# The second layer's second feed-forward chunk: from a plain product to seven products, with its weights' sums made behind the root's logarithm

## The chip, the cores and the metric

The kernel runs on one core of a Trainium2 chip. The metric is the device time of one execution in microseconds (us). TensorE (PE) multiplies, VectorE (DVE) and ScalarE (ACT) do the elementwise work, GpSimd (POOL) issues the adding transfers, SyncE (SP) issues all other loads and stores.

## The reference, cut to what matters

An encoder of two layers runs on 768 tokens (512 and 256) of width 1024. Behind each layer's mixer comes a feed-forward part:

```python
h = rms_norm(x, norm_mlp[i])
x = x + jnp.square(jax.nn.relu(h @ mlp_w_up[i])) @ mlp_w_down[i]
```

`mlp_w_up` is 1024 x 4096, everything is float32. `rms_norm` multiplies each token by one over the root of its mean square; the kernel applies that factor (`rstd`) behind the product, since it is the same for all of a token's columns.

## The kernel before

All data stand with channels on the 128 partitions and the 768 tokens along the free dimension. A float32 operand is split in two parts, a rounded high part (`hi`, made by ACT) and the rest (`lo`, made by DVE as source minus `hi`), and a product is the sum of three: hi by hi, hi by lo, lo by hi. A low part can also be made by an adding transfer: ACT writes -hi into `lo`, and a transfer from POOL's queue adds the source to it (`Weights7.added`).

The feed-forward part works in 16 chunks `u` of 256 hidden units, and `mlp` lists its jobs: chunks 0, 1 and 2, then `down` products and further chunks in turns. A chunk has two raw tiles of weights of 128 x 1024, `raw[0]` and `raw[1]`, loaded by SP into three `wraw` buffers. A chunk's product has two forms:

- *plain* (`up_plain`, `up_begun`): two outputs `p1` and `p2` of 768 tokens, each 48 matmuls of 384 columns, 96 in all. `up_begun` is the first chunk; its two outputs enclose the sum of squares `ss`, the logarithm `ln` and the steps to `rstd`.
- *seven products* (`up`): weights and inputs are each taken as 2 x 2 blocks, and seven products of 12 matmuls do what eight do. They need sums of the blocks: `sums32` and `sums14` make the weights' (two DVE steps each, into tiles `sum0` and `sum1`), `Sums` made the inputs' earlier (`t`). The seven are, in order, `w11` (into bank `a`), `s3` (`b`), `s2` (into `a` again), `w12` (`c`), `s1`, `w22` (`d`) and `s4`. Between `w11` and `s2` ACT copies `a` to `c`, since the `w12` product continues from that, while `s2` goes on adding to `a`.

`PLAIN` says for each layer how many chunks are plain, 2 and 2. `Weights7.high` makes a group's high part on ACT and `low` the low part on DVE. Groups are `direct` (w11, w12), `second` (w21, w22), `s32` (s3, s2; tiles `zhi`, `zlo`), `s14` (s1, s4) and `w22` (`vhi`, `vlo`). PSUM has four banks of tag A, two of B and two of C.

What becomes of a chunk behind its product stands in `pend`, a list of steps that `late` issues inside the next chunk: squaring `y`, the parts `act` of it, and its sums `t`. Inside `mlp` the order on PE, DVE and ACT is the order in which this code is written (`manual_schedule`), and each engine works strictly through its own list. Multiplication by `rstd` with the rectifier is `rectified`, a DVE step `y<-p,rstd_mlp`.

Of the kernel before, what the change touches and what calls it, by code (L numbers as in the profile page):

```python
# [11 lines left out]
F32 = mybir.dt.float32  # L12
F32R = mybir.dt.float32r
AF = mybir.ActivationFunctionType
ALU = mybir.AluOpType
# [32 lines left out]
def trunk_kernel(ctx: ExitStack, tc: tile.TileContext, a: dict, out: bass.AP):  # L48
    nc = tc.nc
    act, dve, pe = nc.scalar, nc.vector, nc.tensor  # L50
# [31 lines left out]
    def split(hi, lo, src):  # L82

        first = act.activation(hi, src, AF.Copy)
        dve.tensor_tensor(lo, src, hi.bitcast(F32), ALU.subtract)
        return first.ins
# [23 lines left out]
    def fresh(name="mm", n=1, tag=None):  # L110

        nonlocal shift
        if tag is None:
            shift += 1
            tag = "ACAB"[shift % 4]
        return bank(tag, name) if n == 1 else [bank(tag, name) for _ in range(n)]

    def both(name="mm", tag=None):

        return [t[:, :H] for t in fresh(name, 2, tag)]  # L120
# [29 lines left out]
    def slot(i, name, dt=F32R, n=T):  # L150

        return (slots if i < 32 else more).tile([P, n], dt, tag=f"S{i}", name=name)

    def big(name, dt=F32):

        nonlocal turn
        if more is None:
            return tmp.tile([P, T], dt, tag="t", name=name)
        turn += 1
        return tmp.tile([P, T], dt, tag=f"q{turn % 6}", name=name, bufs=1)  # L160
# [174 lines left out]
    class Sums:  # L335
# [26 lines left out]
        def low(self, i):  # L362
            hi, lo = self.t[i]
            dve.tensor_tensor(lo[:], (self.q1, self.q2)[i][:], hi[:].bitcast(F32), ALU.subtract)

        def added(self, i):

            hi, lo = self.t[i]
            act.activation(lo[:], hi[:].bitcast(F32), AF.Copy, scale=-1.0)
            nc.gpsimd.dma_start(lo[:], (self.q1, self.q2)[i][:], accum_op=ALU.add)  # L370
# [34 lines left out]
    class Weights7:  # L405
# [44 lines left out]
        def added(self, group):  # L450

            self.high(group)
            self.due.remove(group)
            hi, lo, _ = self.parts[group]
            act.activation(lo[:], hi[:].bitcast(F32), AF.Copy, scale=-1.0)
            src = self.src[group != "direct"]
            nc.gpsimd.dma_start(lo[:], src[:, src.shape[1] - lo.shape[1] :], accum_op=ALU.add)

        def low(self, group):
            if group not in self.due:  # L460
# [477 lines left out]
    def up_chunk(l, u):  # L938
        f = 4 * (u // 2) + u % 2
        return Weights7(a["up"][l, f], a["up"][l, f + 2], plain=u < PLAIN[l])  # L940


    PLAIN = 2, 2

    def weave(*chains):

# [98 lines left out]
    def mlp(l, norm, nxt, w, places, early, product=None, begun=None):  # L1045
# [11 lines left out]
        def squared(t):  # L1057
            act.activation(t[:], t[:], AF.Square)  # L1058

        def acts_of(u, y1, y2, rest):  # L1060

            own = places[7 * (u % 2) : 7 * (u % 2) + 7]
            e = Acts(y1, y2, own, groups[u // 2], u % 2)
            if u < 2 * NG - 2:
                return [
                    lambda: squared(rest),
                    lambda: e.highx(0),
                    lambda: (e.highx(1), e.lowx(0), e.lowx(1), e.t13()),
                    e.t42,
                    lambda: e.high(0),  # L1070
                    lambda: e.high(1),
                    lambda: e.low(0),
                    lambda: e.low(1),
                ]

            def whole(i, q):
                hi, lo = slot(own[2 * i], "act"), slot(own[2 * i + 1], "act")
                split(hi[:], lo[:], q[:])
                groups[u // 2].setdefault("whole", {})[u % 2, i] = hi[:], lo[:]

            return [lambda: squared(rest), lambda: whole(1, y2), lambda: whole(0, y1)]
# [22 lines left out]
        def up_begun(u, w, make, then):  # L1104


            nonlocal r
            v, parts, *sums = begun
            ps = [both(f"p{i + 1}", "A") for i in range(2)]
            if sums:  # L1110
                return up_first(ps, w, v, parts, *sums)
            plain_block(ps[0], 0, w)
            ss = norm.sum_squares(psum, parts=parts, tag="C")
            logs, newton, result = norm.rstd_steps(psum, ss)
            logs()
            v.split("direct")
            newton()
            result()
            r = norm.r
            y = [big(f"y{i + 1}") for i in range(2)]  # L1120
            for i in range(2):
                if i:
                    plain_block(ps[1], 1, w)
                for o in range(2):
                    rectified(y[i], ps[i][o], H * o, H * o + H, ALU.max)
                if i == 0:
                    squared(y[0])
            pend.extend(acts_of(u, *y, y[1]))
            return v

        def up_first(ps, w, v, parts, s1):


            nonlocal r
            plain_block(ps[0], 0, w, range(4))
            ss = norm.sum_squares(psum, parts=parts, tag="C")
            plain_block(ps[0], 0, w, range(4, KB))
            plain_block(ps[1], 1, w)
            logs, newton, result = norm.rstd_steps(psum, ss)
            logs()  # L1140
            s1.t13()
            s1.t42()
            s1.high(0)
            s1.high(1)
            newton()
            s2 = norm.copied(2, 6)
            result()
            r = norm.r
            v.high("direct")
            s1.low(0)  # L1150
            s1.low(1)
            s2.t13()
            s2.high(0)
            v.low("direct")
            v.added("second")
            s2.t42()
            s2.high(1)
            s3 = norm.copied(3, 7)
            s2.low(0)
            s2.low(1)  # L1160
            y = [big(f"y{i + 1}") for i in range(2)]
            for i in range(2):
                for o in range(2):
                    rectified(y[i], ps[i][o], H * o, H * o + H, ALU.max)
                if i == 0:
                    s3.t13()
                    s3.high(0)
                    squared(y[0])
                    s3.added(0)
                    s3.t42()  # L1170
                    s3.high(1)
            pend.extend(acts_of(0, *y, y[1]))
            aside.append(lambda: s3.added(1))
            return v
# [93 lines left out]
        def up(u, w, make, then):  # L1268


            first = u == PLAIN[l]
            w.low("s32")
            w.split("s14")
            if not first:
                late()
            v = make()
            seven = isinstance(v, Weights7)
            a = bank("A", "a")[:, :H]
            product7(a, w, "w11", xs, True)
            if not first:  # L1280
                late()
            c = bank("A" if first else "C", "c")[:, :H]
            act.activation(c, a, AF.Copy)
            late(5 if first else 1)
            w.split("w22")
            late()
            b = bank("A" if first else "B", "b")[:, :H]
            product7(b, w, "s3", xs, True)
            p = big("p")[:, :H]
            act.activation(p, b, AF.Copy)  # L1290
            if seven:
                v.sums32()
            product7(a, w, "s2", xs, False)
            d = bank("B", "d")[:, :H]
            act.activation(d, a, AF.Copy)
            late(2)
            if seven:
                v.sums14()
                v.high("s32")
            late()  # L1300
            product7(c, w, "w12", xs, False)
            if seven:
                v.high("direct")
            product7(a, w, "s1", xs, False)
            y1, y2 = big("y1"), big("y2")
            dve.tensor_tensor(y2[:, H:], a, p, ALU.add)  # L1306
            rectified(y1, c, 0, H, ALU.max)
            late()
            if seven:
                v.low("direct")  # L1310
            else:
                v = [then(0)]
            product7(d, w, "w22", xs, False)
            if seven:
                v.added("w22")
            dve.tensor_tensor(y2[:, :H], d, p, ALU.add)
            rectified(y2, y2[:], 0, T, ALU.min)
            squared(y2)
            product7(a, w, "s4", xs, False)
            rectified(y1, a, H, T, ALU.max)  # L1320
            pend.extend(acts_of(u, y1, y2, y1))
            return v
# [74 lines left out]

        ups = [(up if u >= PLAIN[l] else up_plain, u) for u in range(2 * NG)]
        if begun:
# [585 lines left out]
```

## Time and profile before

| | |
|---|---|
| time, median of 3 runs | 1660.08 us (1659.68 to 1662.16) |
| profiled execution | 1661.51 us, its span 1659.5 us |
| granted TensorE clock, mean | 0.996 |
| busy share | PE 99%, DVE 83%, ACT 57%, POOL 4% |
| layer 2, first chunk | PE from 1098.1 us |
| layer 2, second chunk | PE from 1115.5 to 1132.2 us |
| layer 2, third chunk | PE from 1132.2 to 1146.9 us |

The profile is of one execution. Times of rows count from the start of its span. A row of an engine's order in time gives start, length, engine, source line, operation, output<-input, shape and how many follow each other; in brackets stands how long the engine was idle ahead of it and what ended that. The line is that of `kernel.py` before. PE's rows overlap, as one matmul starts before the last has ended.

### The profile page before, as it was taken

The numbers are of one execution on the slowest core, as the hardware profiler recorded it, in microseconds if no ns is written. First come the engines' busy times: TensorE is split into PE (matmuls) and PEld (weight loads), VectorE is DVE, ScalarE is ACT, GpSimd is POOL, SyncE is SP. The second block draws the span as 40 slices with busy tenths as digits, with TensorE's granted clock in tenths as the row PEclk, the third lists the DMA queues.
The fourth block names the chain that finished last, engine by engine and source line by source line (L and its number), as shares of the span: only waits on it lengthen the run. The fifth ranks groups of instructions, "written<-read, shape, count | busy, mean of one in ns | idle before, by whom it ended". The sixth has DMA issues, their size and how long they took to land.

```text
span 1659.5 us, 24297 instructions
## 1 busy us (share of the span) xinstructions
PE 1637.6 (99%) x9414; PEld 1587.3 (96%) x9414; DVE 1380.8 (83%) x2242; ACT 948.5 (57%) x1508; POOL 71.7 (4%) x104
## 2 busy tenths in 40 slices
PE   8999999999999999999999999999999999999997
PEld 7988789999999999999999999999999999999986
DVE  7598888898889889877888777778889888988776
ACT  7377766865556556545654434555555655655554
POOL 0211000000000000000000000000000000000000
PEclk9999999999999999999999999999999999999998
DMA  8755322443233333242312222112333323333222
GB/s 267 199 154 149 87 64 83 121 109 87 83 86 96 96 96 91 71 122 69 98 62 77 76 77 76 64 64 73 87 96 96 95 87 79 90 96 108 69 87 99
DMA packets 55476, 161.11 MB, mean 97 GB/s; under 512 B 7056, under 2 KB 10128, under 8 KB 55360
## 3 DMA queue, kind: packets, MB, share of 16 engines
q1 hardware_dynamic: 45184, 139.89, 26.4%
q0 software_dynamic: 10176, 19.67, 6.7%
q8 instruction: 74, 1.21, 0.3%
q14 instruction: 42, 0.34, 0.1%
HBM read 138.82 MB, written 10.48 MB: 90 GB/s over the span
## 4 chain that ended last, share of the span: by engine, by line
PE 88%; DVE 7%; ACT 4%; issue 1%; DMA 0%; DVEq 0%; SPq 0%; ACTq 0%
PE a L486 33%; PE mm L131 10%; PE mm L140 8%; PE b L486 8%; PE d L486 5%; PE c L486 5%; PE B L486 4%; PE C L486 4%; PE gate L140 3%; PE pt L760 1%; PE p L1096 1%; PE p L1199 1%; PE gate L131 1%; PE O L770 1%; PE O L771 1%
## 5 line engine op out<-in xcount | busy, mean ns | idle before, releaser
L486 PE MATMUL a<-xs,whi 128*128 128x384 f32 x624 | 121.8, 337 | 0.0
L444 ACT ACTIVATE vhi<-wraw 128x512 fp32r<-128x512 f32 x67 | 42.2, 631 | 132.3 <-PE B L486 87.9
L486 PEld LDWEIGHTS a<-xs,whi 128*128 128x128 f32 x624 | 110.0, 188 | 0.2 <-DVE y L1306 0.2
L486 PE MATMUL a<-t,zhi 128*128 128x384 f32 x536 | 109.1, 337 | 0.0
L486 PE MATMUL a<-t,whi 128*128 128x384 f32 x536 | 108.8, 336 | 0.0
L486 PE MATMUL b<-t,zhi 128*128 128x384 f32 x536 | 108.7, 336 | 0.0
L1341 DVE TENSOR_TENSOR x<-x,a 128x384 f32<-128x384 f32 x112 | 62.1, 554 | 55.3 <-PE a L486 55.3
L486 PE MATMUL a<-act,whi 128*128 128x384 f32 x448 | 96.5, 337 | 0.0
L486 PEld LDWEIGHTS a<-t,whi 128*128 128x128 f32 x536 | 94.9, 188 | 0.0
L486 PEld LDWEIGHTS b<-t,zhi 128*128 128x128 f32 x536 | 94.9, 188 | 0.0
L486 PEld LDWEIGHTS a<-t,zhi 128*128 128x128 f32 x536 | 94.8, 188 | 0.0
L464 DVE TENSOR_TENSOR wlo<-wraw,whi 128x1024 fp32r<-128x1024 f32 x70 | 85.2, 1218 | 7.9 <-ACT whi L444 7.9
L444 ACT ACTIVATE whi<-sum 128x1024 fp32r<-128x1024 f32 x67 | 70.6, 1054 | 27.0 <-PE a L486 22.7
L464 DVE TENSOR_TENSOR wlo<-sum,whi 128x1024 fp32r<-128x1024 f32 x67 | 81.8, 1220 | 5.1 <-ACT whi L444 5.1
L1058 ACT ACTIVATE y<-y 128x768 f32<-128x768 f32 x64 | 53.7, 839 | 54.4 <-DVE y L1055 54.3
L464 DVE TENSOR_TENSOR zlo<-sum,zhi 128x1024 fp32r<-128x1024 f32 x67 | 81.5, 1217 | 0.0
L140 PE MATMUL mm<-xs_mix,whi 128*128 128x512 f32 (+1 forms) x320 | 81.0, 341 | 0.0
L486 PEld LDWEIGHTS a<-act,whi 128*128 128x128 f32 x448 | 79.8, 188 | 0.0
L444 ACT ACTIVATE whi<-wraw 128x1024 fp32r<-128x1024 f32 x72 | 75.7, 1051 | 7.0 <-PE C L486 7.0
L444 ACT ACTIVATE zhi<-sum 128x1024 fp32r<-128x1024 f32 x67 | 70.9, 1058 | 11.9 <-DVE sum L420 11.0
L486 PE MATMUL a<-xs,wlo 128*128 128x384 f32 x312 | 67.1, 336 | 0.0
L358 ACT ACTIVATE t<-y 128x768 fp32r<-128x768 f32 x56 | 45.7, 838 | 34.9 <-DVE y L349 34.4
(345 smaller groups left out, 4558.4 us busy)
## 6 DMA issues: line engine op xcount, KB each, us to landing
wraw<-in_up SPq DMA_DIRECT2D x64, 512.0 KB, 3.9
wraw<-in_down SPq DMA_DIRECT2D x64, 512.0 KB, 4.2
wraw<-in_w_in SPq DMA_DIRECT2D x24, 512.0 KB, 3.5
wraw<-in_gate SPq DMA_DIRECT2D x16, 512.0 KB, 3.4
vlo<-in_up POOLq DMA_DIRECT2D x28, 256.0 KB, 5.6
vlo<-in_down POOLq DMA_DIRECT2D x28, 256.0 KB, 6.0
pj<-pjs SPq DMA_DIRECT2D x16, 384.0 KB, 2.8
wraw<-in_w_q SPq DMA_DIRECT2D x8, 512.0 KB, 4.6
```

Source lines behind the costliest of these rows:

```text
L131: pe.matmul(t, lhsT=w, rhs=x[:, o:e], start=first and i == 0 and j == 0, stop=last and i == n - 1 and j == 2)
L140: pe.matmul(ps[:, o:e], lhsT=w, rhs=x[:, o:e], start=i == 0 and j == 0, stop=i == n - 1 and j == 2,)
L358: act.activation(t[0][:], (self.q1, self.q2)[i][:], AF.Copy)
L444: act.activation(hi[:], src, AF.Copy)
L464: dve.tensor_tensor(lo[:], src, hi[:].bitcast(F32), ALU.subtract)
L486: pe.matmul(ps, lhsT=a, rhs=b, start=start and i == 0, stop=i == len(terms) - 1, skip_group_check=True)
L760: pe.transpose(pt[:, h * P : (h + 1) * P], lg[h // 2][:, h % 2, b * P : (b + 1) * P], ident[:],)
L770: pe.matmul(O[:], lhsT=v, rhs=ph[:], start=b == 0, stop=False)
L771: pe.matmul(O[:], lhsT=v, rhs=pl[:], start=False, stop=b == nk - 1)
L1058: act.activation(t[:], t[:], AF.Square)
L1096: pe.matmul(ps[o], lhsT=wt[:, c], rhs=xs[f"x{h + 1}{1 + o}"][m][part], start=k == 0 and j == 0, stop=k == KB - 1 and j == 2,)
L1341: dve.tensor_tensor(t[:, o : o + H], t[:, o : o + H], f, op)
```

## The change

In the second layer one chunk is plain in place of two: the second chunk now goes through `up`. `up_begun` now makes that chunk's weights: behind the logarithm's steps the high part of `direct`, the first sums, their high part, the `w22` group by an adding transfer, and the low part of `direct`; behind the rectifying steps the low part of `s32` and the second sums. Its output `p2` moves from banks A to banks B. Inside `up` the second chunk makes the low part of the third chunk's `s32` by an adding transfer from the tile `sum` (`sum_added`). The flag `first`, which gave the first chunk in seven products other banks and an order of its own, now holds in layer 1 alone.

```diff
+        def sum_added(self):
+            self.high("s32")
+            self.due.remove("s32")
+            hi, lo, src = self.parts["s32"]
+            act.activation(lo[:], hi[:].bitcast(F32), AF.Copy, scale=-1.0)
+            nc.gpsimd.dma_start(lo[:], src, accum_op=ALU.add)
...
-    PLAIN = 2, 2
+    PLAIN = 2, 1
...
     def up_begun(u, w, make, then):
-            ps = [both(f"p{i + 1}", "A") for i in range(2)]
+            ps = [both(f"p{i + 1}", "A" if sums else "AB"[i]) for i in range(2)]
...
             logs()
-            v.split("direct")
+            v.high("direct")
+            v.sums32()
+            v.high("s32")
+            v.added("w22")
+            v.low("direct")
             newton()
             result()
...
+            v.low("s32")
+            v.sums14()
             pend.extend(acts_of(u, *y, y[1]))
...
     def up(u, w, make, then):
-            first = u == PLAIN[l]
+            first = u == PLAIN[l] == 2
...
                 v.sums14()
-                v.high("s32")
+                if u == 1:
+                    v.sum_added()
+                else:
+                    v.high("s32")
```

The order on ACT from the last step of the logarithm (`ln<-y`) to the first copy of a bank (`c<-a`). `wraw` is a raw tile, `sum` a tile of sums. Before, that copy belongs to the third chunk:

```order
L259 ACTIVATE ln<-y 128x768
L444 ACTIVATE zhi<-wraw 128x1024
L1058 ACTIVATE y_11274<-y_11274 128x768
L1058 ACTIVATE y_11275<-y_11275 128x768
L390 ACTIVATE act<-y_11274 128x384
L394 ACTIVATE act<-y_11275 128x768
L444 ACTIVATE whi<-wraw 128x1024
L358 ACTIVATE t_11405<-y_11274 128x768
L444 ACTIVATE zhi<-sum 128x1024
L444 ACTIVATE vhi<-wraw 128x512
L455 ACTIVATE vlo<-vhi 128x512
```

Now, where the copy belongs to the second chunk:

```order
L444 ACTIVATE whi<-wraw 128x1024
L444 ACTIVATE zhi<-sum 128x1024
L444 ACTIVATE vhi<-wraw 128x512
L455 ACTIVATE vlo<-vhi 128x512
L1066 ACTIVATE y_11286<-y_11286 128x768
L444 ACTIVATE whi<-sum 128x1024
L1066 ACTIVATE y_11287<-y_11287 128x768
L390 ACTIVATE act<-y_11286 128x384
L1297 ACTIVATE c<-a 128x384
```

Four steps on weights have moved to right behind the logarithm, and `whi<-sum`, a squaring and a part `act` stand ahead of the copy.

The order on DVE from the same place (`v<-ss`, behind the logarithm), before:

```order
L257 TENSOR_SCALAR v<-ss 128x384 x2
L464 TENSOR_TENSOR zlo<-wraw,zhi 128x1024
L263 SCALAR_TENSOR_TENSOR v<-ln,v 128x768
L270 SCALAR_TENSOR_TENSOR rstd_mlp_11272<-v,y 128x768
L1055 SCALAR_TENSOR_TENSOR y_11274<-p_11200,rstd_mlp_11272 128x384
L1055 SCALAR_TENSOR_TENSOR y_11274<-p_11201,rstd_mlp_11272 128x384
L1055 SCALAR_TENSOR_TENSOR y_11275<-p_11202,rstd_mlp_11272 128x384
L1055 SCALAR_TENSOR_TENSOR y_11275<-p_11203,rstd_mlp_11272 128x384
L419 TENSOR_TENSOR sum<-wraw 128x512
```

And now:

```order
L419 TENSOR_TENSOR sum<-wraw 128x512
L420 TENSOR_TENSOR sum<-sum,wraw 128x512
L472 TENSOR_TENSOR wlo<-wraw,whi 128x1024
L263 SCALAR_TENSOR_TENSOR v<-ln,v 128x768
L270 SCALAR_TENSOR_TENSOR rstd_mlp_11284<-v,y 128x768
L1063 SCALAR_TENSOR_TENSOR y_11286<-p_11202,rstd_mlp_11284 128x384
L1063 SCALAR_TENSOR_TENSOR y_11286<-p_11203,rstd_mlp_11284 128x384
L1063 SCALAR_TENSOR_TENSOR y_11287<-p_11204,rstd_mlp_11284 128x384
L1063 SCALAR_TENSOR_TENSOR y_11287<-p_11205,rstd_mlp_11284 128x384
L472 TENSOR_TENSOR zlo<-sum,zhi 128x1024
L424 TENSOR_TENSOR sum<-wraw 128x512
L425 TENSOR_TENSOR sum<-wraw,sum 128x512
```

The first two sums have moved ahead of the steps to `rstd`, and the low part `zlo` and the second sums stand right behind the four rectifying steps.

## Prediction

> **What bounds the kernel now.** I read the page's first part, then the chain that ended last, then the three engines' instructions in order of time around the change, then what stalls the matrix engine anywhere.
>
> ```profile
> PE 1637.6 (99%) x9414; PEld 1587.3 (96%) x9414; DVE 1380.8 (83%) x2242; ACT 948.5 (57%) x1508; POOL 71.7 (4%) x104
> 1115.68 16.69 PE p L1199 x96
> 1132.37 2.10 PE a L486 x12
> 1134.47 2.09 PE b L486 x12
> ```
>
> The first line is the busy time of each engine, the others are pieces of the chain (start, length, what). PE is the bound, and around the change the chain is PE without a gap: the second chunk in 96 plain matmuls (L1199), then the third chunk in products of 12 matmuls. A matmul removed here is time saved, and a wait of PE here is time lost, one for one, because no later transfer or gap takes it up.
>
> **The change, part by part.** *Matmuls.* 96 become 84. At 16.69 us for the 96 and 2.095 for 12 (the two lengths above), 16.69 - 7 x 2.095 = 2.02 us is saved, if PE never waits. (`project_add` still splits the second raw half of this chunk, of which a quarter is used and is made again: both kernels do it ahead of the logarithm, so it costs nothing new.) But a product of twelve can start only when its bank is free and its weights are there, and a plain block of 48 asked for that a quarter as often. So I follow the two other queues from the root's logarithm on. The rows of before, first ACT, then DVE, the last five from the third chunk, as prices:
>
> ```profile
> 1112.16 0.84 ACT L259 ACTIVATE ln<-y 128x768 f32<-128x768 f32 x1
> 1112.91 1.04 ACT L444 ACTIVATE zhi<-wraw 128x1024 fp32r<-128x1024 f32 x1
> 1124.88 0.61 ACT L444 ACTIVATE vhi<-wraw 128x512 fp32r<-128x512 f32 x1
> 1125.52 0.64 ACT L455 ACTIVATE vlo<-vhi 128x512 fp32r<-128x512 f32 x1
> 1134.51 0.47 ACT L1283 ACTIVATE c<-a 128x384 f32<-128x384 f32 x1 [1.21 <-PE a L486]
> 1134.89 0.84 ACT L1058 ACTIVATE y<-y 128x768 f32<-128x768 f32 x1
> 1135.63 0.51 ACT L390 ACTIVATE act<-y 128x384 fp32r<-128x384 f32 x1
> 1136.05 0.83 ACT L394 ACTIVATE act<-y 128x768 fp32r<-128x768 f32 x1
> ...
> 1111.06 1.02 DVE L257 TENSOR_SCALAR v<-ss 128x384 f32<-128x384 f32 x2
> 1113.99 1.23 DVE L464 TENSOR_TENSOR zlo<-wraw,zhi 128x1024 fp32r<-128x1024 f32 x1 [1.91 <-ACT zhi L444]
> 1115.13 0.95 DVE L263 SCALAR_TENSOR_TENSOR v<-ln,v 128x768 f32<-128x768 f32 x1
> 1116.12 0.96 DVE L270 SCALAR_TENSOR_TENSOR rstd_mlp<-v,y 128x768 f32<-128x768 f32 x1
> 1117.11 1.95 DVE L1055 SCALAR_TENSOR_TENSOR y<-p,rstd_mlp 128x384 f32<-128x384 f32 x4
> 1118.98 0.68 DVE L419 TENSOR_TENSOR sum<-wraw 128x512 f32<-128x512 f32 x1
> 1119.69 0.69 DVE L420 TENSOR_TENSOR sum<-sum,wraw 128x512 f32<-128x512 f32 x1
> ...
> 1127.32 0.68 DVE L424 TENSOR_TENSOR sum<-wraw 128x512 f32<-128x512 f32 x1
> 1127.92 0.68 DVE L425 TENSOR_TENSOR sum<-wraw,sum 128x512 f32<-128x512 f32 x1
> 1136.21 0.55 DVE L400 TENSOR_TENSOR act<-y,act 128x384 fp32r<-128x384 f32 x1
> 1136.91 0.96 DVE L403 TENSOR_TENSOR act<-y,act 128x768 fp32r<-128x768 f32 x1
> 1137.78 0.55 DVE L348 TENSOR_TENSOR y<-y 128x384 f32<-128x384 f32 x1
> ```
>
> *First sums moved behind the logarithm.* DVE was idle for 1.91 us before the zlo at 1113.99, and the two steps of the first sum (0.68 + 0.69) fit there: 1112.0 to 1113.4. The direct weights' high part takes the place of zhi at 1112.91 and its low part the place of zlo. ACT adds zhi<-sum, vhi and vlo (1.05 + 0.61 + 0.64) and is done at 1116.1, before it can square at 1118.1. So root, rectifying steps and everything before them stay at their times: this part costs nothing, its cover being the 1.91 us gap on DVE and ACT's wait for DVE; without it, 1.4 us.
>
> *Bank.* The first product `a` starts at 1115.5 and ends at 1117.6. `b` takes a bank that the first chunk's second block fills, freed by the third of the four rectifying steps (they start at 1117.11, 0.47 apart, 0.55 each): 1118.6. PE waits 1.0 us.
>
> *Low part of the first sum.* It stands behind the four rectifying steps: 1119.0 + 1.2 = 1120.2. PE is through b's eight matmuls with the high part at 1118.64 + 8 x 0.1745 = 1120.04 and waits 0.2 more; b is done at 1120.95.
>
> *The copy c<-a.* The next product adds to `a`, so it waits until ACT has copied `a`. That copy stands on ACT behind whi<-sum, which waits for DVE's second pair of sums, queued behind zlo: 1120.1 + 0.60 + 0.68 = 1121.4 (the pitch and length of the rows at 1127.32). From there by the rows above: whi<-sum about 1.05, to 1122.5; then at the pitch from 1134.89 to 1136.05 (0.74 + 0.42) a squaring and act; the copy runs 1123.55 to 1124.0. PE, ready at 1120.95, waits 3.1 us. In before the same copy found ACT idle (1.21 in brackets), since the weights were ready sooner.
>
> Waits: 1.0 + 0.2 + 3.1 = 4.35 with the unrounded hundredths; against 2.02 saved, +2.33 us where the third chunk begins.
>
> *The adding transfer of the next sum.* It takes 1.22 off DVE in the third chunk and puts a second ACT pass (about 1.05) and a 512 KB transfer in its place, one more issue on POOL ahead of the next vlo, none on SP, whose order is unchanged. The nearest transfers:
>
> ```profile
> wraw<-in_up SPq DMA_DIRECT2D x64, 512.0 KB, 3.9
> wlo<-in_up POOLq DMA_DIRECT2D x2, 512.0 KB, 6.1
> t<-q POOLq DMA_DIRECT2D x2, 384.0 KB, 3.9
> DMA to landing us min/median/max: 4.1/5.7/7.8
> 1126.57 0.87 POOL L457 DMA_DIRECT2D vlo<-in_up  x1 [282.01 <-DVE zlo L464]
> 1132.20:1146.90 14.70, 14.70 (x86) 14.70 (x86) 13.84 (x20) 9.16 (x13) 0.82 (x1) 1.00 0.14 48
> ```
>
> The last row is the third chunk: DVE 13.84 busy in 14.70, so a late DVE stays late. DVE goes on at 1122.5 with the second sum's low part (1.23), the two act parts (0.55, 0.96), four steps like the one at 1137.78 (0.58 with their gaps) and the next sum (1.4), 6.5 us, and waits some 0.3 for ACT's second act part: it has the sum at 1129.3; ACT makes zhi and -zhi by 1131.5; POOL issues 0.4 later, as after vlo's end at 1126.16. Landing takes 3.9 (from SBUF, but 384 KB) to 7.8 us, I take 5.2 (3.9 scaled by size): 1137.1. PE wants it at 1134.55 + 2.1 + 1.4 = 1138.05. Cost zero, 1.65 at the slow end. What waits for it beside PE is DVE's next sum into the same tile, at about 1143. SP's load of the third chunk's second raw half now waits for DVE's step of 1120.1 to have read that buffer: 1120.8 + 3.9 = 1124.7, wanted at 1127.9, so 3 us of slack. In the third chunk c<-a comes at 1139.1 by the same walk, PE wants it at 1138.75: 0.35 more, +2.7 in all, if PE is at full clock.
>
> *The clock.* A PE that waits loses more than the wait. Rows of PE's order of time and of stretches of the span (after the engines' busy times: granted clock, DMA):
>
> ```profile
> 202.48 0.79 PE L140 MATMUL mm<-aos,whi 128*128 128x512 f32 x1 [1.56 <-DVE aos L85]
> 203.07 0.63 PE L140 MATMUL mm<-aos,wlo 128*128 128x512 f32 x1
> 203.50 0.84 PE L140 MATMUL mm<-aos,whi 128*128 128x512 f32 x2
> 12.33 0.52 PE L140 MATMUL mm<-p0l,whi 128*128 128x512 f32 x2
> 12.68 0.52 PE L140 MATMUL mm<-p0h,wlo 128*128 128x512 f32 x2
> 195.40:198.80 3.40, 2.82 (x18) 2.11 (x17) 3.36 (x9) 3.35 (x7) 0.00 (x0) 1.00 0.57 126
> 198.83:202.24 3.41, 2.10 (x9) 1.16 (x8) 3.29 (x12) 2.23 (x6) 0.00 (x0) 1.00 0.66 181
> 202.24:205.65 3.41, 3.17 (x9) 2.59 (x10) 3.41 (x12) 1.97 (x7) 0.00 (x0) 0.50 0.39 152
> 1646.00:1649.40 3.40, 1.18 (x5) 0.50 (x4) 2.38 (x8) 2.40 (x4) 0.00 (x0) 1.00 0.20 77
> 1649.40:1650.20 0.80, 0.77 (x2) 0.10 (x1) 0.67 (x2) 0.00 (x0) 0.00 (x0) 0.56 0.00 0
> ```
>
> After a wait of 1.56 us the clock was 0.50 for 3.41 us. The 3.41 us before the drop had PE busy for 2.10; a stretch with 2.82 did not drop; at the end one with 1.18 did. And the drop went away after 3.41 us with 3.17 busy. Between 202.24 and 1649.5 lie 1447.25 us, which is 424 such stretches: a fixed grid. On this grid a boundary falls at 202.24 + 270 x 3.4133 = 1123.84, and the 3.41 us before it have PE busy for about 0.5. So I expect the clock at half from 1123.84 to 1127.25, while PE works from 1124.07 on. At half clock a 512-column matmul took 0.43 (203.07 to 203.50); at full clock 512 and 256 columns took 0.35 together (12.33 to 12.68), 0.235 for the 512: a factor of 1.83. 3.18 us at half clock lose 3.18 x (1 - 1/1.83) = 1.45 us. Bounds: 0, if the wait were too short to count; 2.6, if the grid lies so that the drop falls in mid-wait and the next stretch is too idle to lift it. I take 1.45, since the grid follows from rows of this execution. The slower PE gives ACT and DVE the time that the 0.35 was short of, and the transfer its slack, so both fall away.
>
> The Trainium skill, "TensorE: Matmul & The Clock Gate", Part 1, has the clock fall to half only after a whole idle window of about 3.4 us; the longest wait here is 3.1, so by that rule it would stay full and the sum be +2.7. The trace does not agree: 1.56 us of waiting was enough, with PE busy for 2.10 of the 3.41.
>
> **Sum.** -2.02 + 4.35 + 1.45 = +3.8 us. The profiled execution took 1661.51 us (span 1659.5 and 2.0 around it) and would become 1665.3; it stands 1.4 above the median of the three runs, 1660.08. On the median: 1663.9.
>
> **Rivals.** *A: the clock stays full.* Only the waits count, with the 0.35 that returns: +2.7, 1662.8. For it: the longest wait stays below 3.41. Against it: the row at 202.48. Chance 0.13, which is also that of the skill's rule.
> *B: the clock stays at half for two stretches*, 2.6 lost in place of 1.45, or the adding transfer lands late by up to 1.65: +4.9 to +5.5, about 1665.1. For it: a run can lie otherwise on the grid, and a 512 KB transfer from SBUF is not in the trace. Against it: the grid computed above, and 1 us of slack. 0.19.
> *C: it ends on the other side.* c<-a is the place. If ACT could copy `a` by 1121.8 in place of 1124.0, the waits would fall to about 2.0 and the change would break even; with the copy at 1119.7 and the bank free, the whole 2.0 would be gained, 1658.1. For that the second pair of sums would have to be made before the rectifying steps, or the copy stand ahead of whi<-sum. In the order it does neither. 0.05, most of it between 1658 and 1660.
> *D: the forecast*, waits and one stretch of half clock: 0.63.
>
> **How the numbers follow.** The range 1661.9 to 1665.7 takes in A at its lower side and B's usual size at the upper, with about 1 us for what three runs scatter (1659.68 to 1662.16); C and the worst of B, some 0.15, are left out. A measurement of this kernel tells about 0.2% or 3.3 us from no change. D at +3.8 is over it in 7 of 10, B nearly always, A in one of four: 0.44 + 0.18 + 0.03 = 0.65 slower; 0.02 faster, from C; 0.33 within.
>
> **What would show it.** In the profile after: 84 product matmuls in the second chunk; PE idle of about 1.0 before its first `b`, ended by DVE's rectifying step, 0.2 by zlo, about 3.1 before the next `a`, ended by ACT's c<-a; a clock of 0.5 for one stretch of 3.4 us from there; the third chunk's start 3.8 us later than 1132.2; no wait of PE for the transfer into zlo. I am wrong if ACT copies `a` before DVE's second pair of sums, if the clock stays at 1.00 there, or if PE waits on the transfer.

## The result, and the profile after

The changed kernel takes 1667.02 us (median of 6 runs, 1663.97 to 1668.05), the kernel before 1661.10 us in the 6 runs that go with it (1659.68 to 1662.77). The ratio is 1.0033, with a 95% interval of 1.002 to 1.0046: slower, by 0.2 to 0.46%. The sign and the place were forecast, the time was not: 1663.9 with an upper end of 1665.7. Of the 3.1 us between forecast and result the changed place holds 0.3; 2.2 was in the number that the forecast was added to.

First the changed place. The chain that ended last (start, length, what), which was PE without a gap in the kernel before, now runs through ACT and DVE until PE starts its third product:

```profile
1117.50 1.95 DVE y L1063 x4
1119.45 1.13 DVE zlo L472
1120.58 0.60 DVE sum L424
1121.19 0.61 DVE sum L425
1121.88 1.06 ACT whi L444
1122.94 0.73 ACT y L1066
1123.67 0.41 ACT act L390
1124.09 0.39 ACT c L1297
1124.51 3.88 PE a L494 x12
1128.39 2.09 PE c L494 x12
1130.48 2.10 PE a L494 x12
```

Each piece is what released the next, or stood ahead of it on its engine (pieces under 0.1 us are left out). Four rectifying steps, the low part of the first sums, the second sums, ACT's `whi<-sum`, a squaring, a part `act` and the copy stand between PE and its third product, and that product takes 3.88 us where the next two take 2.09 and 2.10. In order of time, PE (L494 is the product, L486 before):

```profile
1115.84 1.56 PE L494 MATMUL a<-xs,whi 128*128 128x384 f32 x8
1117.24 0.86 PE L494 MATMUL a<-xs,wlo 128*128 128x384 f32 x4
1119.13 1.63 PE L494 MATMUL b<-t,zhi 128*128 128x384 f32 x8 [1.04 <-DVE y L1063]
1120.64 0.97 PE L494 MATMUL b<-t,zlo 128*128 128x384 f32 x4
1124.51 2.93 PE L494 MATMUL a<-t,zhi 128*128 128x384 f32 x8 [2.91 <-ACT c L1297]
```

and ACT and DVE in the same stretch:

```profile
1121.88 1.06 ACT L444 ACTIVATE whi<-sum 128x1024 fp32r<-128x1024 f32 x1 [2.48 <-DVE sum L425]
1122.85 0.83 ACT L1066 ACTIVATE y<-y 128x768 f32<-128x768 f32 x1
1123.58 0.51 ACT L390 ACTIVATE act<-y 128x384 fp32r<-128x384 f32 x1
1123.99 0.47 ACT L1297 ACTIVATE c<-a 128x384 f32<-128x384 f32 x1
...
1119.37 1.22 DVE L472 TENSOR_TENSOR zlo<-sum,zhi 128x1024 fp32r<-128x1024 f32 x1
1120.50 0.69 DVE L424 TENSOR_TENSOR sum<-wraw 128x512 f32<-128x512 f32 x1
1121.10 0.69 DVE L425 TENSOR_TENSOR sum<-wraw,sum 128x512 f32<-128x512 f32 x1
```

`a` was complete at about 1118, and ACT did nothing from 1119.4 to 1121.88; the copy that PE needed stood in ACT's queue behind `whi<-sum`, which waited for DVE. The list of ACT's order before, under the change, ends three steps short of the copy; there too `whi<-sum` stood ahead of it:

```profile
1132.24 1.06 ACT L444 ACTIVATE whi<-sum 128x1024 fp32r<-128x1024 f32 x1 [3.95 <-PE p L1199]
```

But DVE had finished those sums at 1128.6, so `whi<-sum` was done before `a` was, and the copy was in time. What is new is that the sums come late, and that a squaring and a part `act` now stand ahead of the copy too.

The granted clock by stretches of the changed kernel (behind the engines' busy times; the last three numbers are clock, DMA share, GB/s):

```profile
1121.61:1124.51 2.90, 0.00 (x0) 0.00 (x0) 1.72 (x3) 2.63 (x5) 0.00 (x0) 0.99 0.73 270
1124.44:1127.85 3.41, 3.34 (x10) 3.34 (x11) 2.76 (x5) 1.16 (x3) 0.00 (x0) 0.50 0.23 88
1127.85:1136.62 8.77, 8.77 (x52) 8.77 (x52) 7.92 (x13) 6.18 (x8) 0.90 (x1) 1.00 0.30 54
```

Half clock for one stretch of 3.41 us, from 0.07 us before PE resumes. The second chunk takes from 1115.84 to 1136.62, 20.78 us against 16.69 before (1115.52 to 1132.21): +4.09. The third takes 14.66 (14.67 before). From the first `down` to PE's last two products it takes 502.37 us, 502.32 before. So up to there the change costs 4.1 us, all in one chunk.

### The profile page after: what moved, and what is told of

The parts are those of the page before. It is cut to its first block, busy times and chain, and to the rows that moved or that the text cites. A ratio compares the mean times of both kernels' runs of the same rounds, so it can differ in the third digit from the quotient of the medians.

```text
span 1664.5 us, 24291 instructions
## 1 busy us (share of the span) xinstructions
PE 1638.4 (98%) x9402; PEld 1587.1 (95%) x9402; DVE 1385.7 (83%) x2248; ACT 954.0 (57%) x1516; POOL 73.5 (4%) x106
## 4 chain that ended last, share of the span: by engine, by line
PE 86%; DVE 8%; ACT 4%; issue 1%; DMA 0%; DVEq 0%; SPq 0%; ACTq 0%
PE a L494 34%; PE mm L131 10%; PE mm L140 8%; PE b L494 8%; PE d L494 5%; PE c L494 5%; PE B L494 4%; PE C L494 4%; PE gate L140 3%; PE pt L768 1%; PE gate L131 1%; PE O L778 1%; PE O L779 1%; DVE t L364 1%; PE S L733 1%
## 5 line engine op out<-in xcount | busy, mean ns | idle before, releaser
L494 PE MATMUL a<-xs,whi 128*128 128x384 f32 x640 | 124.9, 337 | 0.0
L494 PE MATMUL a<-t,zhi 128*128 128x384 f32 x544 | 112.0, 340 | 2.9 <-ACT c L1297 2.9
L494 PEld LDWEIGHTS a<-xs,whi 128*128 128x128 f32 x640 | 112.9, 188 | 0.3 <-DVE y L1323 0.2
L494 PE MATMUL b<-t,zhi 128*128 128x384 f32 x544 | 110.4, 336 | 1.0 <-DVE y L1063 1.0
L494 PE MATMUL a<-t,whi 128*128 128x384 f32 x544 | 110.3, 336 | 0.0
L494 PEld LDWEIGHTS a<-t,zhi 128*128 128x128 f32 x544 | 97.2, 190 | 3.2 <-ACT c L1297 3.2
L494 PEld LDWEIGHTS b<-t,zhi 128*128 128x128 f32 x544 | 96.2, 188 | 1.3 <-issue 1.3
L494 PE MATMUL a<-act,whi 128*128 128x384 f32 x448 | 96.5, 337 | 0.0
L494 PEld LDWEIGHTS a<-t,whi 128*128 128x128 f32 x544 | 96.3, 188 | 0.0
L494 PEld LDWEIGHTS a<-act,whi 128*128 128x128 f32 x448 | 79.8, 188 | 0.0
L494 PE MATMUL a<-xs,wlo 128*128 128x384 f32 x320 | 68.8, 336 | 0.0
```

The source lines that it names most:

```text
L494: pe.matmul(ps, lhsT=a, rhs=b, start=start and i == 0, stop=i == len(terms) - 1, skip_group_check=True)
```

## The other part of the difference: two groups of times

The times of one and the same kernel are not scattered about a middle. The 73 runs of the kernel before that went with all these experiments fall into one group at 1658.96 to 1660.79 (32 runs, median 1659.91) and one at 1661.23 to 1663.20 (41 runs, median 1662.25); the 12 of the changed kernel at 1663.93 to 1664.16 (3) or at 1666.05 to 1668.05 (9, median 1667.21). The mean clock of each run is on record for all but six of the 73: it is 0.997 in all 29 of the earlier group and 0.996 in all 38 of the later, and in the changed kernel 0.996 in the 3 and 0.995 in the 9. One stretch of 3.41 us at half clock takes 0.001 off the mean over 1660 us, so the groups differ by what one such stretch takes. The profiles show it at 202 us, 900 us ahead of the change, where PE waits 1.55 us for `aos`: in some executions that wait costs a stretch of half clock, in others none.

The clock changes on a grid. In the profile of after it falls at 202.84, 1124.44 and 1653.51 us, which are 270 and 155 stretches of 3.413 us apart. Stretches of this grid around the wait, of the changed kernel and then of experiment e2, whose code is the same up to there:

```profile
199.43:202.84 3.41, 1.86 (x9) 1.22 (x9) 3.30 (x12) 2.23 (x7) 0.00 (x0) 1.00 0.65 174
202.84:206.25 3.41, 3.41 (x11) 2.84 (x12) 3.41 (x12) 1.59 (x7) 0.00 (x0) 0.50 0.32 119
...
198.27:201.68 3.41, 2.31 (x9) 1.38 (x9) 3.29 (x13) 2.23 (x5) 0.00 (x0) 1.00 0.63 166
201.68:205.09 3.41, 2.90 (x17) 2.55 (x17) 3.41 (x11) 2.25 (x10) 0.00 (x0) 1.00 0.47 185
```

In the first the wait lies in one stretch (PE busy 1.86 of 3.41), in the second a boundary of the grid cuts it in two (2.31 and 2.90). All ten profiled executions agree:

| profile | clock after the wait at 202 us | second chunk starts | span |
|---|---|---|---|
| before | 0.50 | 1115.52 | 1659.5 |
| before again (e5) | 0.50 | 1116.67 | 1660.2 |
| after | 0.50 | 1115.84 | 1664.5 |
| after again (e1) | 0.50 | 1116.56 | 1664.9 |
| e6 | 0.50 | 1115.84 | 1664.4 |
| e2 | 1.00 | 1113.83 | 1661.0 |
| e3 | 1.00 | 1114.21 | 1661.6 |
| e4 | 1.00 | 1113.48 | 1661.5 |
| e7 | 1.00 | 1114.19 | 1659.0 |
| e8 | 1.00 | 1114.65 | 1660.9 |

With the drop at 202 us the second chunk begins at 1116.1 on average, without it at 1114.1. Where the grid lies differs between executions of one kernel: the drop came at 202.24 us in one profile of before and at 203.78 in the other, with the wait ending at 202.48 and 203.43. Group by group the change costs 4.06 us (1659.91 to 1663.97, 3 runs) and 4.96 us (1662.25 to 1667.21). The medians stand further apart, by 5.9, because 9 of the 12 runs of after, but 41 of 73 of before, fell into the later group. With 12 runs that can be chance, and the code ahead of 202 us is the same.

## Experiments

Times stand beside runs of the kernel before on the same chip. The length that tells the theories apart is taken inside one execution, from the start of the second chunk to the first `down`, so that the two groups don't enter: 31.36 us in both profiles of before, 35.44 in that of after.

**e1: the changed kernel again,** without an edit.

> The changed kernel once more, unaltered, for its size. The prediction's theory (waits of PE and one stretch of half clock in the second chunk, nothing elsewhere): the time from the first matmul of the second chunk to the end of PE's work is 4.1 us longer than before, and the span likewise, so about 1665 us against 1661. The rival (something outside the second chunk also costs, since six runs put it at +5.9): 5.5 to 6 us again in the median of the runs.

1666.79 us against 1661.55, ratio 1.0031 (1.0019 to 1.0043). The length is 35.49, the second chunk 20.83, the waits 1.05 and 2.91. What the chunk costs repeats to 0.05 us, while its start moved by 0.7 us and the run times by 3.6.

**e2: the copy ahead of the second sums' split.**

```diff
-            w.split("s14")
-            late(2)            # around v = make(), product7(a, w, "w11")
             v = make()
             product7(a, w, "w11", xs, True)
             act.activation(c, a, AF.Copy)
+            w.split("s14")     # for l == 1, u == 1 alone
+            late(2)
```

> Second chunk: ACT copies a to c ahead of the high part of the second sums, the squaring and the act part. Theory: PE's wait of 2.9 us for c<-a goes, and the half clock right behind it; b still waits 1.0. DVE's queue is then the bound: y<-a,p comes at about 1131.9 as before, so the product s4 waits some 2.0 to 2.4 us instead; the time falls by about 2 us, or 0.7 if that new wait drops the clock. Rival (the copy was late for another reason, or the matmuls behind it are slow by themselves): no change, the wait stays.

1665.10 us, ratio 1.0022 (1.0013 to 1.0031); length 34.53. PE no longer waits for `c<-a`. It waits at the chunk's last product instead, for DVE's `y<-a,p`, and there the clock falls (0.91 on the mean of the chunk, the last row's third number from the end):

```profile
1127.19 0.87 PE L494 MATMUL d<-t,vlo 128*128 128x384 f32 x4
1129.94 2.80 PE L494 MATMUL a<-xs,whi 128*128 128x384 f32 x8 [1.88 <-DVE y L1328]
1132.54 1.31 PE L494 MATMUL a<-xs,wlo 128*128 128x384 f32 x4
...
1113.83:1133.69 19.86, 16.92 (x86) 16.02 (x85) 18.24 (x27) 11.41 (x16) 1.77 (x2) 0.91 0.37 88
```

So ACT's queue was the cause of the 2.91 us. Two thirds of it come back behind DVE, which had `y<-a,p` behind four sums for the next chunk and a step `t`, and the half-clock stretch moves along: this product takes 3.75 us.

**e3: PE kept busy during the wait.** 16 matmuls into a bank that nobody reads, between the second and the third product; nothing else differs.

```diff
+            if l == 1 and u == 1:
+                spare = bank("A", "spare")[:, :H]
+                for i in range(16):
+                    wt, (xh, _) = w.w["w11"][0], xs["x11"][i % 4]
+                    pe.matmul(spare, lhsT=wt[:, P * (i % 4) : P * (i % 4) + P], rhs=xh, start=i == 0, stop=i == 15)
             product7(a, w, "s2", xs, False)
```

> Sixteen matmuls of 384 columns into an unused bank stand between the products b and s2 of the second chunk, in PE's wait of 2.9 us; their result is read by nobody. Theory of the clock: PE stays busy, the granted clock stays 1.00, s2 takes 2.1 us in place of 3.7, and the time falls by 1.6 us. Rival (s2 is slow because of the transfers that run at 350 GB/s there, or because of DVE and ACT): s2 stays at 3.7 and the time stays, or rises by 0.1.

1663.41 us, ratio 1.0019 (1.001 to 1.0027); length 34.59.

```profile
1119.84 2.96 PE L1307 MATMUL spare<-xs,whi 128*128 128x384 f32 x16
1122.91 1.67 PE L494 MATMUL a<-t,zhi 128*128 128x384 f32 x8
1124.41 0.86 PE L494 MATMUL a<-t,zlo 128*128 128x384 f32 x4
...
1114.21:1133.50 19.29, 18.12 (x101) 17.32 (x101) 17.25 (x26) 11.46 (x16) 1.77 (x2) 1.00 0.32 82
```

The third product starts 8.70 us after the chunk, as in after (8.67), and takes 2.20 in place of 3.72; the clock is 1.00 over the whole chunk (the last row), while the transfers move about as much over it as in after (82 GB/s, 86 there). With the same copy at the same distance, idleness alone costs 1.5 us. The third chunk then waits 0.36 for its own `c<-a`, where the forecast had 0.35 for a PE at full clock, and takes 15.30; the net gain is 0.85.

**e4: the next sum's low part by DVE,** as before the change, the rest unchanged.

```diff
-                if u == 1:
-                    v.sum_added()
-                else:
-                    v.high("s32")
+                v.high("s32")
```

> The low part of the third chunk's first sums by DVE, as before, in place of ACT's second pass and the adding transfer. Theory: the transfer and its saving are both hidden, 0 within 0.3 us. Rival (the transfer pays for itself, since DVE is the late engine): slower by up to 1.2 us, with PE waiting for zlo or for c<-a in the third chunk.

1665.25 us, ratio 1.0029 (1.0017 to 1.004); length 35.51, second chunk 20.84, waits 1.05 and 2.91. The adding transfer neither costs nor brings anything here. The median is lower than that of after because 3 of its 6 runs fell into the earlier group (1663.74 to 1664.24).

**e5: the kernel before again.**

> The kernel before, unaltered, profiled a second time. Theory 1 (the times of one kernel come in two groups about 2.5 us apart, because PE's wait of 1.55 us at about 202 us costs a stretch of half clock in some executions and not in others): if this execution has the clock at 1.00 from 202 to 206, its span is about 1657.5 and its second chunk begins at 1113.4 to 1114.3; if the clock is 0.50 there, the span is about 1659.5 to 1660.5 and the chunk begins at 1115.5 to 1116.6. From the second chunk's start to the third stage's start (first `down`) it takes 31.36, as in the first profile. Theory 2 (the scatter lies around the span or behind the changed place): the second chunk begins at the same time whatever the clock at 202.

1662.57 us (11 runs) against 1660.95 (22 runs) of the very same kernel, ratio 1.0007 (0.9998 to 1.0015): medians of one kernel can stand 1.6 us apart. In the profile the clock is 0.50 behind the wait at 202, the chunk starts at 1116.67 (expected 1115.5 to 1116.6), the length is 31.36. No profile of the kernel before is of the earlier group; of these 11 runs, the three at 1659.62 to 1660.05 have a mean clock of 0.997 and the other eight 0.996, and five profiles of other kernels with the same code ahead of the change show the execution without the drop.

**e6: `b` in a free bank.**

```diff
-            b = bank("A" if first else "B", "b")[:, :H]
+            b = bank("A" if first or (l == 1 and u == 1) else "B", "b")[:, :H]
```

> The changed kernel, with the second chunk's product `b` in a free bank, so that it doesn't wait for the rectifying steps. Theory 1 (the waits stand in series behind ACT's copy c<-a, whose time is set by DVE and ACT alone): the 1.05 us in front of `b` goes, but its low-part half then waits for zlo, and PE still cannot start the third product before the copy; the copy stands at the same distance from the chunk's start, so the chunk keeps its 20.8 us (20.5 to 20.9) and the time is the changed kernel's, 1664 or 1667. Theory 2 (each wait adds its own length): 1.05 less, 19.7 us.

1666.47 us, ratio 1.0031 (1.0018 to 1.0043); the second chunk takes 20.68 us.

```profile
1117.93 1.55 PE L494 MATMUL b<-t,zhi 128*128 128x384 f32 x8
1120.65 0.95 PE L494 MATMUL b<-t,zlo 128*128 128x384 f32 x4 [1.16 <-DVE zlo L472]
1124.52 2.93 PE L494 MATMUL a<-t,zhi 128*128 128x384 f32 x8 [2.92 <-ACT c L1297]
```

The wait of 1.04 is gone, one of 1.16 for `zlo` stands within `b`, and the third product starts 8.68 us after the chunk, as before. The waits are in series: with the first taken away, ACT's copy still sets when the third product starts.

**e7: DVE and ACT reordered** in the second and third chunk, to find what the change could bring. The third chunk's `s32` is split by DVE again, without the adding transfer. The lines that are taken from their old places are left out here.

```diff
             act.activation(c, a, AF.Copy)
+            w.split("s14")                       # l == 1, u in (1, 2), here and below
+            late(2)
...
             act.activation(d, a, AF.Copy)
+            v.high("direct")
+            v.sums32()
+            v.high("s32")
             late(2)
...
             rectified(y1, c, 0, H, ALU.max)
             v.low("direct")
+            v.low("s32")
...
             rectified(y1, a, H, T, ALU.max)
+            v.sums14()
+            late(2)
```

> The changed kernel with DVE and ACT reordered in the second and third chunk: c<-a ahead of the chunk's last weight sums, the next chunk's first weights split earlier and by DVE (no adding transfer), y<-a,p ahead of the next second pair of sums, those and two input sums behind the chunk's last rectifying step. The work is the same but for the transfer's 1.2 us on DVE. Theory 1 (the order cost the time, DVE's work just fits): the waits for c<-a and for y<-a,p go, that of 1.05 in front of `b` stays without a drop of the clock; second chunk 15.8 us, third 14.7 to 15.2, together 30.5 to 31.0 against 31.36 of the kernel before: 0.4 to 0.9 faster than it. Theory 2 (DVE is the bound of the two chunks: it has about 30.4 us of work in them against PE's 29.3, with waits of its own): PE stalls at another place of the third chunk or at the first `down`, and the two take 31.4 or more.

1662.59 us against 1660.95, ratio 1.001 (1.0001 to 1.0018). The two chunks take 30.90 us, 0.46 less than before. Then the first `down` waits:

```profile
1147.19 0.68 PE L494 MATMUL b<-t,zhi 128*128 128x384 f32 x3
1149.07 0.44 PE L494 MATMUL b<-t,zhi 128*128 128x384 f32 x1 [1.19 <-DVE t L364]
...
1114.19:1130.42 16.23, 15.18 (x85) 14.47 (x85) 14.65 (x22) 9.17 (x14) 0.87 (x1) 1.00 0.29 82
1130.42:1145.09 14.67, 14.67 (x86) 14.67 (x85) 14.50 (x22) 10.31 (x16) 0.90 (x1) 1.00 0.33 89
```

The last two rows are the two chunks (length; PE, weight loads, DVE, ACT, POOL busy): DVE works 14.50 of the third chunk's 14.67 us. A chunk in seven products gives PE 2.02 us less, and DVE more to do: over the two chunks it works 27.02 of 31.36 us in before and 29.15 of 30.90 in e7. In the third chunk DVE is full, and what it does later PE may wait for later; e8 puts that to the test.

**e8: the third chunk's input sums first,** in the kernel of e7, ahead of the next second sums, to take away that 1.19.

```diff
-            v.sums14()
             late(2)
+            v.sums14()                           # u == 2 alone
```

> The reordered kernel, with the two input sums of the third chunk (t) ahead of the next second pair of sums on DVE, so that the first `down` finds them. Theory 1 (in the reordered kernel only the 1.19 us at `down` gives back what the two chunks gain, 30.9 against 31.36 us): that wait falls to 0.0 to 0.3, nothing new comes in its place, and the time is 0.2 to 0.6 below the kernel before, too little to be told from it. Theory 2 (DVE is full, so whatever is put first makes another thing late): a wait of about 1 us appears at another product of `down`, and the time stays at or above the kernel before.

1664.71 us against 1660.42, ratio 1.0026 (1.0015 to 1.0038). The wait for `t` is gone, and a longer one stands at the next product of `down`:

```profile
1152.66 0.96 PE L494 MATMUL a<-t,zhi 128*128 128x384 f32 x4 [2.48 <-ACT C L1370]
...
1150.44 1.06 ACT L444 ACTIVATE whi<-sum 128x1024 fp32r<-128x1024 f32 x1 [2.62 <-DVE sum L425]
1151.40 0.83 ACT L1066 ACTIVATE y<-y 128x768 f32<-128x768 f32 x1
1152.13 0.85 ACT L1370 ACTIVATE C<-a 128x384 f32<-128x384 f32 x2
```

It is the change's own wait once more: the copy of a bank behind `whi<-sum`, that behind DVE's second sums. No version here is faster than the kernel before.

## Why the prediction was right and wrong

*Matmuls, right.* Seven products take 14.66 us in the third chunk of after; 2.02 saved.

*First sums behind the logarithm, right.* The rectifying steps start 1.66 us after the chunk (1.59 before).

*The three waits, right.* Forecast 1.0, 0.2 and 3.1, or 4.35 in all. Measured from start to start, the third product begins 8.67 us after the first. In seven products at full speed it is 4.19, as in the third chunk of before (`a` at 1132.37 in the prediction's rows, and then):

```profile
1136.56 2.09 PE a L486 x12
```

The difference is 4.48: 1.20 for the bank, 0.11 for `zlo` and 3.17 for the copy. (The brackets, 1.04 and 2.91, count from the end of a matmul, which the next one otherwise overlaps.) e2 and e6 show that the copy is the link that sets it.

*The adding transfer, right.* It landed in 5.6 us (5.2 estimated), PE did not wait, and e4 without it has the same length.

*The clock, right in kind, 0.2 short.* Forecast one half-clock stretch from 1123.84, 3.18 us of it with PE at work, for 1.45. The drop came 0.07 us before PE resumed, so PE worked in 3.34 of its 3.41 us. At the forecast's factor of 1.83 that loses 1.5; the product lost 1.63 (3.72 - 2.09). That the boundary would lie just there was partly luck: it was reckoned on the grid of one execution of before. In the profiles it lay 0.29 us before PE's restart (e6), 0.07 before (after), 0.48 behind (e1) and 0.50 behind (e4). The price hardly depends on it, since the second chunk takes 20.68 to 20.84 us in all four.

*Rivals.* A, the clock that stays full, is refuted here: no wait was longer than 2.92, and the clock fell in after, e1, e4 and e6; in e3, with the wait filled, it did not. The Trainium skill, "TensorE: Matmul & The Clock Gate", Part 1, has the clock fall after an idle window of about 3.4 us. The traces do not agree: at 202 us a wait of 1.54 to 1.56 was enough in five profiles. B did not come about: one stretch of half clock, and no late transfer. C was priced too well: for it to break even the prediction asked for the copy 6.3 us behind the chunk's start. In e2 the copy is done 4.0 us behind it, and the length is still 3.2 us above before, since DVE's `y<-a,p` became the next limit and brought its own half clock.

*The step that failed: "On the median: 1663.9".* The working gave +3.8 for a profiled execution of 1661.51, so 1665.3, and then moved it to the median of three runs, 1660.08. That execution had the half-clock stretch at 202 us: its row, 202.24:205.65 at 0.50, served as a price, and the prediction did not ask whether that stretch is there in every run. Of the three runs, 1659.68 and 1660.08 are of the group without it, 1662.16 of that with it. The "about 1 us for what three runs scatter" was really a second value 2.3 us higher (1662.25 - 1659.91). Counted in the later group, to which 9 of 12 runs of after belong, the forecast is 1662.25 + 3.8 = 1666.1 against 1667.21; in the earlier, 1659.91 + 3.8 = 1663.7 against 1663.97. The highest run of the later group, 1663.20, and 3.8 make 1667.0, which is where a range that held both groups would have had to end.

Of what is left in the later group, 1.1 us, 0.3 is the changed chunk (4.09 for 3.78). In the profiles some 0.5 of the remaining 0.8 lies at the very end. From the first `down` to the end of the span, after has 513.20 and 512.86 us in its two profiles, before 512.64 and 512.21; up to PE's last two products these are the same to 0.1. The two products take 1.22 and 0.91 us in after, 0.97 and 0.70 in before, as more or less of them falls into the kernel's last stretch at half clock. The stretch behind DVE's last step takes 4.59 and 4.54, against 4.33 and 4.19; the cause of that stays open.

## What to carry to other kernels

Before adding a forecast to a median, sort the run times: if they fall into two groups, find which one the profiled execution belongs to, and forecast each group by itself. When work moves from the full engine to one that is 83% busy, look at that engine in the stage itself and follow each engine's list in its order: a small copy that PE waits for must not stand behind a step that waits for a third engine. Where several waits stand in series behind one late step, taking an earlier one away changes nothing, as e6 showed.

## What the runs showed of the hardware

A wait of the same length costs a half-clock stretch or not, depending on where it falls on the 3.41-us grid: that at 202 us (1.54 to 1.56 us) did in five of the ten profiles, that of 2.48 us in e8 did not. There a boundary of the grid, reckoned back from that execution's drop at 1653.02, lies at about 1151.27 and cuts it:

```profile
1147.85:1151.27 3.42, 2.32 (x12) 1.70 (x11) 2.49 (x4) 0.83 (x1) 0.00 (x0) 1.00 0.62 102
1151.27:1154.68 3.41, 2.02 (x11) 2.03 (x12) 2.51 (x3) 2.97 (x7) 0.00 (x0) 1.00 0.74 290
1154.68:1158.10 3.42, 3.42 (x21) 3.42 (x21) 3.42 (x6) 2.50 (x3) 0.00 (x0) 1.00 0.00 0
```

The exact condition stays open. Around 202 us the five stretches with PE busy for 1.86, 1.86, 1.87, 2.01 and 2.10 us were followed by half clock; those with 2.28 (e7) and 2.31 (e2, e3, e8) were not. But the stretch with 2.02 in the row above was not either, so PE's busy time by itself doesn't decide it near 2.0.

The two groups follow the drop at 202 us in all ten profiles, and the mean clock of every run on record has the one stretch more in the later group. But no run took that wait away by itself. That the wait at 202 us makes the groups is thus an agreement of profiles and clocks, not an experiment.
